# Weight subtractions, index lookup and the pace of routing in a two-layer encoder kernel

## The chip, the core and the metric

The kernel runs on one core of one Trainium2 chip, as one program without loops. The metric is the device time of one execution in microseconds (us); the time given is the median of the timed runs. Engines are named as in the profile: PE (TensorE, matrix products), PEld (its weight loads), DVE (VectorE), ACT (ScalarE), POOL (GpSimd) and SP (which issues the DMA loads of weights).

## What is computed

Two layers over 256 tokens of width 1024. Each layer runs four kinds of attention on the tokens (the *mixers*) and then a feed-forward part called PEER, which picks experts by keys. The change lies almost wholly in PEER:

```python
def peer_ffn(u, wq, keys, u_tab, v_tab):
    q = (u @ wq).reshape(b, s, PEER_HEADS, 2, PEER_DKEY // 2)
    scores = jnp.einsum('bshpk,hpnk->bshpn', q, keys).astype(jnp.float32)
    sub_s, sub_i = lax.top_k(scores, PEER_TOPK)
    cand_s = (sub_s[..., 0, :, None] + sub_s[..., 1, None, :]).reshape(...)
    cand_i = (sub_i[..., 0, :, None] * PEER_NKEYS + sub_i[..., 1, None, :]).reshape(...)
    top_s, pos = lax.top_k(cand_s, PEER_TOPK)
    eidx = jnp.take_along_axis(cand_i, pos, axis=-1)
    gates = jax.nn.softmax(top_s, axis=-1)
    ...
        h = jax.nn.gelu(jnp.einsum('td,thkd->thk', ut, ue).astype(jnp.float32), approximate=False)
        w = (gt * h).astype(ut.dtype)
        return jnp.einsum('thk,thkd->td', w, v_tab[it])
```

There are 8 heads, 128 keys on each of two sides (so 16384 experts), and 16 experts are kept per head and token.

## The kernel before

**Split products.** Every float32 product with a weight is made of three products in a faster format: a value is split into `hi` and `lo`, and hi x hi, lo x hi and hi x lo are added. `stream` (L102) loads one weight block of 128 x 1024 into `raw` (three buffers, `raw_load` L91), ACT writes `hi` (L97), and an engine subtracts, `lo = raw - hi` (L98). `hi` and `lo` have three buffers each. Which engine subtracts is decided in `stream`: `share["every"]` is 0 in the mixers (always DVE), 3 in routing and in the output sum (every third block goes to POOL) and 2 in gating (every second block):

```python
        eng = eng or (G if share["every"] and share["n"] % share["every"] == 0 else V)
```

`w_out_blocks` (L774) splits eight blocks of the attention's output weight per layer, four of them with POOL (`wol`).

**PEER in three stages** (`peer`, L833). The kernel doesn't gather experts. It computes the hidden value of all 16384 experts, 128 tiles of 128, and sets the gate of those not chosen to zero.

1. *Routing* (`routing` L852). A call of `hidden` (L996) computes two tiles of experts: two weight blocks of `in_pu`, 24 matmuls of 256 columns each (L288 to L290). Between the calls stand steps of routing: `project` and `score` for 16 pairs of head and side (tile `sc`), then `top16` of 128 scores (L1110 to L1115, into `subs` and `iu`, from there to `subi`), and then, for each half `t` of the tokens, 100 candidate sums per head (`cand`), `top16` of them (`tops`, `pos`), the *lookup* and a softmax. Each step yields a cost. A loop (L1016 to L1023) adds a credit of 3.2 per call of `hidden` and hands out steps until the credit is used up. The costs before are 2.6 for the first projection, `CH` = 1.1 for each of 16 projections, 1.0 for each of 32 top-16, and per half of the tokens twice 0.6, eight times 0.9, 0.5, four times 1.7 + 1.1, 0.5 and 0.5. The costs only set the order in which the program is written; they are no waits.
2. *Lookup*, the part of routing that turns positions among candidates into key numbers (L930 to L941): a position's 4-bit index is compared with 0 to 15 (tile `oh`, one-hot, L933), multiplied by the 16 kept key numbers `subi` (L939) and summed over the 16 (L941, into `res`). One pass does one side for four heads, so there are four passes of 128 x 1024 per half.
3. *Gating* (`gating` L961). For eight tokens at a time it compares both key numbers with 0 to 127 (`a`, L976; `e`, L978) and multiplies `e` by the gates (`b`, two times, L980). PE multiplies `a` and `b` (L985, tile `pC`, eight short matmuls of 128 columns for a batch of four tokens), which gives the gate of each expert; DVE multiplies these into the hidden values `ha` and `hb` (L990), and ACT copies the rest. The 64 batches are spread over the calls of `hidden` that routing left.

After them comes the *output sum* (from L1042): 128 blocks of `in_pv`, split in the same way, twelve matmuls of 512 columns each into `y` (L113 to L115), in the first layer with the next layer's conditioning (`araw`, L152, on DVE) in between.

**What sets the order.** Each engine runs its own list of instructions in order and waits on semaphores. A scheduler places the instructions by the order in which they are written and by its own estimates. A DVE instruction that waits holds up every one behind it, `lo` included.

Of the kernel before, what the change touches and what calls it, by code (L numbers as in the profile page):

```python
# [9 lines left out]
F32 = mybir.dt.float32  # L10
F32R = mybir.dt.float32r
BF = mybir.dt.bfloat16
# [18 lines left out]
GT = 8  # L31
CH = 1.1
GSTEP = 1
BSTEP = 1
GSCALE = 2.0 ** 14


@with_exitstack
def kernel(ctx, tc, T, out):
# [34 lines left out]
    G.iota(iota, pattern=[[1, 128]], base=0, channel_multiplier=0, allow_small_or_imprecise_dtypes=True)  # L74
    iota4 = const([128, 16, 4], BF, "iota4")
    V.tensor_copy(iota4, iota[:, 0:16][:, :, None].to_broadcast([128, 16, 4]))
    mhalf = const([128, 16], F32, "mhalf")
# [21 lines left out]

    share, state = {"every": 0, "n": 0}, {}  # L100

    def stream(src, w=1024, eng=None):  # L102

        raw = raw_load(src, w)
        share["n"] += 1
        eng = eng or (G if share["every"] and share["n"] % share["every"] == 0 else V)
        hi = sp.tile([128, 1024], F32R, name="hi")
        lo = sp.tile([128, 1024], F32R, name="lo")
        split(hi[:, :w], lo[:, :w], raw[:, :w], eng)
        return hi, lo  # L110
# [272 lines left out]
    def mixers(l, u, begun):  # L383
        mpool = tc.tile_pool(name="mix", reuse_waits="tile", bufs=1)
        mx = mpool.__enter__()
        share["every"] = 0
        lambda_init = 0.8 - 0.6 * math.exp(-0.3 * l)
# [386 lines left out]
        with tc.tile_pool(name="mout", reuse_waits="tile", bufs=1) as op:  # L774
            wo = {}

            def w_out_blocks():
                for hh, b in [(hh, b) for b in range(3) for hh in range(2)] + [(0, 3), (1, 3)]:
                    raw = op.tile([128, 1024], F32, name="wraw", bufs=2)
                    nc.sync.dma_start(raw, T["wout"][l, hh, b])  # L780
                    hi = op.tile([128, 1024], F32R, name=f"woh{hh}{b}")
                    lo = op.tile([128, 1024], F32R, name=f"wol{hh}{b}")
                    split(hi, lo, raw, G if b % 2 else V)
                    wo[hh, b] = hi, lo
                    yield
# [49 lines left out]
    def peer(l, u, begun):  # L835
# [16 lines left out]
        def routing(rp):  # L852

            subs = [rp.tile([128, 16, 16], F32, name=f"subs{t}", bufs=1) for t in range(2)]
            subi = [rp.tile([128, 16, 16], BF, name=f"subi{t}", bufs=1) for t in range(2)]
            def project(c):
                if c % 8 == 0:
                    state["keys"] = rp.tile([128, 1024], F32, name="keys", bufs=1)
                    nc.gpsimd.dma_start(state["keys"], T["keys"][l, c // 8])
                if c % 4 == 0:  # L860
                    state["sc"] = [psA("sc").rearrange("p (h n) -> p h n", h=4) for _ in range(2)]
                p = psA()
                if c < 4:
                    for t in range(2):
                        transpose(p[:, t * 128:(t + 1) * 128], qa[:, t, c * 128:(c + 1) * 128])
                else:
                    proj_b(p[:, :S], T["wq"][l, c - 4], u, 8)
                qs = rp.tile([128, S], F32, name="qs")
                A.activation(qs, p[:, :S], AF.Copy)
                return qs  # L870
# [11 lines left out]
            for g in range(4):  # L882
                qs = project(g * 4)
                for i in range(1, 4):
                    yield CH
                    nqs = project(g * 4 + i)
                    score(g * 4 + i - 1, qs)
                    qs = nqs
                yield CH
                score(g * 4 + 3, qs)  # L890
                for t in range(2):
                    iu = rp.tile([128, 4, 16], U32, name="iu")
                    for i in range(4):
                        top16(rp, subs[t][:, g * 4 + i, :], iu[:, i, :], state["sc"][t][:, i, :], 128)
                        yield 1.0
                    V.tensor_copy(subi[t][:, g * 4:g * 4 + 4, :], iu)
            for t in range(2):
# [3 lines left out]
                for h in range(8):  # L901
                    if h % 4 == 0:
# [8 lines left out]
                                        s1[:, :, 0:4][:, :, None, :].to_broadcast([128, 4, 13, 4]), op=ALU.add)  # L911
                        yield 0.6
                    top16(rp, tops[:, h, :], pos[:, h, :], cand[:, h % 4, :], 100)
                    yield 0.9
                au = rp.tile([128, 3, 128], U32, name="au", bufs=1)
# [11 lines left out]
                res = rp.tile([128, 4, 128], F32, name="res", bufs=1)  # L927
                yield 0.5
                for q in range(2):
                    for h4 in range(2):  # L930
                        ks = slice(h4 * 64, h4 * 64 + 64)
                        oh = rp.tile([128, 16, 64], BF, name="oh16", bufs=1)
                        V.tensor_tensor(oh.rearrange("p a (k i) -> p a k i", i=4),  # L933
                                        iota4[:, :, None, :].to_broadcast([128, 16, 16, 4]),
                                        af[:, q, ks].rearrange("p (k i) -> p k i", i=4)[:, None, :, :]
                                        .to_broadcast([128, 16, 16, 4]), op=ALU.is_equal)
                        si = subi[t][:, q::2, :][:, h4 * 4:h4 * 4 + 4, :].rearrange("p h a -> p a h")
                        o4 = oh.rearrange("p a (h k) -> p a h k", h=4)
                        V.tensor_tensor(o4, o4, si[:, :, :, None].to_broadcast([128, 16, 4, 16]), op=ALU.mult)  # L939
                        yield 1.7  # L940
                        V.tensor_reduce(res[:, q, ks], oh.rearrange("p a k -> p k a"), axis=AX.X, op=ALU.add)  # L941
                        yield 1.1
                gv = res[:, 2, :].rearrange("p (h k) -> p h k", h=8)
                V.tensor_tensor(gv, tops, tops[:, :, 0:1].to_broadcast([128, 8, 16]), op=ALU.subtract)
                A.activation(gv, gv, AF.Exp)
                yield 0.5
                gs = rp.tile([128, 8], F32, name="gs")
# [11 lines left out]
                A.activation(rt[:, :, t * 128:(t + 1) * 128], p, AF.Copy)  # L959
                yield 0.5  # L960

# [50 lines left out]
        with tc.tile_pool(name="route", reuse_waits="tile", bufs=2) as rp:  # L1012
            steps, credit = routing(rp), 0.0
            share["every"] = 3
            while steps is not None and state["tiles"] < 128:
                hidden(None)  # L1016
                credit += 3.2 if share["every"] else 2.6
                while credit > 0:
                    c = next(steps, None)
                    if c is None:  # L1020
                        steps = None
                        break
                    credit -= c  # L1023
            if steps is not None:
                for _ in steps:
                    pass
        share["every"] = 2
        with tc.tile_pool(name="gp", reuse_waits="tile", bufs=2) as gp:
# [13 lines left out]
        last = l + 1 == L  # L1042
        share["every"] = 3
        yps = [[psA(f"y{t}{h}") for h in range(2)] for t in range(2)]
# [166 lines left out]
```

## Time and profile before

| | us |
|---|---|
| median of three timed runs | 2518.3 (2515.56 to 2518.84) |
| profiled execution | 2525.81, of it span 2524.0 |
| PE busy | 2390.5 (95%) |
| DVE busy | 1842.1 (73%) |
| ACT busy | 1207.5 (48%) |
| POOL busy | 652.1 (26%) |

A busy time adds up the instructions of an engine. PE's matmuls overlap, so "busy" says that it never stood still, not that it ran at its best pace. Idle time counts against a waiting instruction only after the one before it has ended. In the trace the second layer begins near 1300 us. Its routing runs from about 1680 to 1920, its gating to 2152 and its output sum to 2515; in the first layer routing runs from about 440 to 673, gating to 885, the output sum to 1300.

### The profile page before, as it was taken

The numbers are of one execution on the slowest core, as the hardware profiler recorded it, in microseconds if no ns is written. First come the engines' busy times: TensorE is split into PE (matmuls) and PEld (weight loads), VectorE is DVE, ScalarE is ACT, GpSimd is POOL, SyncE is SP. The second block draws the span as 40 slices with busy tenths as digits, with TensorE's granted clock in tenths as the row PEclk, the third lists the DMA queues.
The fourth block names the chain that finished last, engine by engine and source line by source line (L and its number), as shares of the span: only waits on it lengthen the run. The fifth ranks groups of instructions, "written<-read, shape, count | busy, mean of one in ns | idle before, by whom it ended". The sixth has DMA issues, their size and how long they took to land. (4 is left out here: it accounts for less than half of the span.)

```text
span 2524.0 us, 41444 instructions
## 1 busy us (share of the span) xinstructions
PE 2390.5 (95%) x15844; PEld 2134.6 (85%) x15844; DVE 1842.1 (73%) x3190; ACT 1207.5 (48%) x2114; POOL 652.1 (26%) x348
## 2 busy tenths in 40 slices
PE   7989998998999999899989999999989999999997
PEld 4779987998999988777768899879979999788886
DVE  7766667559899968677577665756798998555556
ACT  3654553444444445445446554734444544444453
POOL 2111012222233333233311110212223334233231
PEclk9999999999999999999999999999999999999999
DMA  8666564554455478787654455635544544566664
GB/s 274 193 179 209 166 215 144 185 176 151 151 160 152 142 253 272 231 277 252 198 163 125 145 159 159 226 109 186 166 137 160 159 151 154 177 189 194 192 214 145
DMA packets 141255, 459.97 MB, mean 182 GB/s; under 512 B 27472, under 2 KB 27488, under 8 KB 141056
## 3 DMA queue, kind: packets, MB, share of 16 engines
q1 hardware_dynamic: 135776, 439.93, 55.1%
q0 software_dynamic: 4848, 16.34, 2.0%
q8 instruction: 124, 2.03, 0.3%
q10 hardware_dynamic: 432, 1.05, 0.1%
q14 instruction: 75, 0.61, 0.1%
HBM read 453.05 MB, written 4.21 MB: 181 GB/s over the span
## 5 line engine op out<-in xcount | busy, mean ns | idle before, releaser
L97 ACT ACTIVATE hi<-raw 128x1024 fp32r<-128x1024 f32 (+2 forms) x705 | 737.8, 1052 | 557.3 <-PE pA L289 163.6
L98 DVE TENSOR_TENSOR lo<-raw,hi 128x1024 fp32r<-128x1024 f32 (+2 forms) x505 | 634.1, 1257 | 305.7 <-ACT hi L97 304.9
L98 POOL TENSOR_TENSOR lo<-raw,hi 128x1024 fp32r<-128x1024 f32 x200 | 507.4, 2537 | 1137.1 <-ACT hi L97 1112.2
L290 PE MATMUL pB<-uh,lo 128*128 128x256 f32 x2048 | 585.7, 286 | 24.8 <-DVE lo L98 24.2
L288 PE MATMUL pB<-uh,hi 128*128 128x256 f32 x2048 | 587.4, 287 | 0.3 <-ACT hi L97 0.3
L289 PE MATMUL pB<-ul,hi 128*128 128x256 f32 x2048 | 580.6, 283 | 0.0
L290 PEld LDWEIGHTS pB<-uh,lo 128*128 128x128 f32 x2048 | 389.1, 190 | 31.5 <-DVE lo L98 27.5
L113 PE MATMUL y<-hi,wh 128*128 128x512 f32 x968 | 385.2, 398 | 12.4 <-ACT hi L97 7.1
L114 PE MATMUL y<-lo,wh 128*128 128x512 f32 x968 | 382.4, 395 | 12.3 <-DVE lo L98 6.5
L288 PEld LDWEIGHTS pB<-uh,hi 128*128 128x128 f32 x2048 | 389.4, 190 | 0.6 <-ACT hi L97 0.5
L289 PEld LDWEIGHTS pB<-ul,hi 128*128 128x128 f32 x2048 | 389.4, 190 | 0.1
L115 PE MATMUL y<-hi,wl 128*128 128x512 f32 x968 | 384.0, 397 | 0.7 <-DVE wl L98 0.7
L98 DVE TENSOR_TENSOR wl<-ha,wh 128x256 fp32r<-128x256 f32 x220 | 146.1, 667 | 171.7 <-ACT wh L97 171.4
L288 PE MATMUL pA<-uh,hi 128*128 128x256 f32 x832 | 240.3, 289 | 0.0
L290 PE MATMUL pA<-uh,lo 128*128 128x256 f32 x832 | 238.5, 287 | 0.9 <-DVE lo L98 0.9
L289 PE MATMUL pA<-ul,hi 128*128 128x256 f32 x832 | 238.3, 286 | 0.0
L114 PEld LDWEIGHTS y<-lo,wh 128*128 128x128 f32 x968 | 184.6, 191 | 56.1 <-DVE lo L98 8.7
L113 PEld LDWEIGHTS y<-hi,wh 128*128 128x128 f32 x968 | 184.5, 191 | 52.3 <-ACT hi L97 8.4
L115 PEld LDWEIGHTS y<-hi,wl 128*128 128x128 f32 x968 | 184.5, 191 | 42.5 <-DVE wl L98 1.5
L97 ACT ACTIVATE wh<-ha 128x256 fp32r<-128x256 f32 x220 | 91.3, 417 | 266.4 <-PE y L114 264.2
L290 PEld LDWEIGHTS pA<-uh,lo 128*128 128x128 f32 x832 | 158.4, 190 | 2.2 <-DVE lo L98 1.1
L288 PEld LDWEIGHTS pA<-uh,hi 128*128 128x128 f32 x832 | 158.5, 191 | 0.7
(312 smaller groups left out, 3646.8 us busy)
## 6 DMA issues: line engine op xcount, KB each, us to landing
raw<-in_pu_dram SPq DMA_DIRECT2D x256, 512.0 KB, 3.6
raw<-in_pv_dram SPq DMA_DIRECT2D x256, 512.0 KB, 4.4
araw<-in_ada_w_dram SPq DMA_DIRECT2D x80, 512.0 KB, 4.9
raw<-in_wgate_dram SPq DMA_DIRECT2D x64, 512.0 KB, 3.6
raw<-in_win_a_dram SPq DMA_DIRECT2D x48, 512.0 KB, 3.7
raw<-in_wbr_dram SPq DMA_DIRECT2D x32, 512.0 KB, 3.8
raw<-in_wq_dram SPq DMA_DIRECT2D x24, 512.0 KB, 3.7
aw<-in_ada_w_dram SPq DMA_DIRECT2D x32, 256.0 KB, 5.8
```

The costliest lines, as they stand in the source:

```text
L97: A.activation(hi, src, AF.Copy)
L98: (eng or V).tensor_tensor(lo, src, hi.bitcast(F32), op=ALU.subtract)
L113: PE.matmul(o, sh, mh, start=first, stop=False)
L114: PE.matmul(o, sh, ml, start=False, stop=False)
L115: return PE.matmul(o, sl, mh, start=False, stop=last).ins
L288: PE.matmul(o[:, ts], hi[:, ws], uh[:, kc, ts], start=kc == 0, stop=False)
L289: PE.matmul(o[:, ts], hi[:, ws], ul[:, kc, ts], start=False, stop=False)
L290: end = PE.matmul(o[:, ts], lo[:, ws], uh[:, kc, ts], start=False, stop=kc == nk - 1)
```

## The change

1. `stream` has no `share` any more: all its blocks are subtracted by DVE, except two at the very start of the program that are given to POOL by name. `w_out_blocks` does the same.
2. The lookup does one side for all eight heads in one pass of 128 x 2048. The key numbers lie twice, side by side, in `subi`, and `iu` is filled in another order, so that the multiply reads pairs. The sum over 16 is made of four additions on halves, the first three in bf16. `oh` shares its memory with `keys`.
3. The credit per call of `hidden` is `RSTEP` = 3.7, and the steps have other costs.

```diff
-CH = 1.1
+CH = 0.3
+RSTEP = 3.7
+OHC = 1.2
-    iota4 = const([128, 16, 4], BF, "iota4")
+    iota16 = const([128, 16, 16], BF, "iota16")
 def stream(src, w=1024, eng=None):
-        share["n"] += 1
-        eng = eng or (G if share["every"] and share["n"] % share["every"] == 0 else V)
 def w_out_blocks():
-                    split(hi, lo, raw, G if b % 2 else V)
+                    split(hi, lo, raw)
 def routing(rp):
-            subi = [rp.tile([128, 16, 16], BF, name=f"subi{t}", bufs=1) for t in range(2)]
+            subi = [rp.tile([128, 2, 128, 2], BF, name=f"subi{t}", bufs=1) for t in range(2)]
-                        top16(rp, subs[t][:, g * 4 + i, :], iu[:, i, :], state["sc"][t][:, i, :], 128)
-                        yield 1.0
-                    V.tensor_copy(subi[t][:, g * 4:g * 4 + 4, :], iu)
+                        top16(rp, subs[t][:, g * 4 + i, :], iu[:, i % 2 * 2 + i // 2, :], state["sc"][t][:, i, :], 128)
+                        yield 1.7
+                    V.tensor_copy(subi[t][:, :, g * 32:g * 32 + 32, :],
+                                  iu.rearrange("p (q h) a -> p q (h a)", q=2)[:, :, :, None]
+                                  .to_broadcast([128, 2, 32, 2]))
-                        yield 0.6
+                        yield 1.7
                     top16(rp, tops[:, h, :], pos[:, h, :], cand[:, h % 4, :], 100)
-                    yield 0.9
+                    yield 1.5
-                yield 0.5
+                yield 1.6
                 for q in range(2):
-                    for h4 in range(2):
-                        ks = slice(h4 * 64, h4 * 64 + 64)
-                        oh = rp.tile([128, 16, 64], BF, name="oh16", bufs=1)
-                        V.tensor_tensor(oh.rearrange("p a (k i) -> p a k i", i=4),
-                                        iota4[:, :, None, :].to_broadcast([128, 16, 16, 4]),
-                                        af[:, q, ks].rearrange("p (k i) -> p k i", i=4)[:, None, :, :]
-                                        .to_broadcast([128, 16, 16, 4]), op=ALU.is_equal)
-                        si = subi[t][:, q::2, :][:, h4 * 4:h4 * 4 + 4, :].rearrange("p h a -> p a h")
-                        o4 = oh.rearrange("p a (h k) -> p a h k", h=4)
-                        V.tensor_tensor(o4, o4, si[:, :, :, None].to_broadcast([128, 16, 4, 16]), op=ALU.mult)
-                        yield 1.7
-                        V.tensor_reduce(res[:, q, ks], oh.rearrange("p a k -> p k a"), axis=AX.X, op=ALU.add)
-                        yield 1.1
+                    oh = rp.tile([128, 8, 16, 16], BF, name="oh16", tag="keys", bufs=1)
+                    V.tensor_tensor(oh, iota16[:, None, :, :].to_broadcast([128, 8, 16, 16]),
+                                    af[:, q, :].rearrange("p (h k) -> p h k", h=8)[:, :, None, :]
+                                    .to_broadcast([128, 8, 16, 16]), op=ALU.is_equal)
+                    yield OHC
+                    ov = oh.rearrange("p h a (k i) -> p (h a) k i", i=2)
+                    V.tensor_tensor(ov, ov, subi[t][:, q, :, None, :].to_broadcast([128, 128, 8, 2]), op=ALU.mult)
+                    yield OHC
+                    for n in (8, 4, 2):
+                        V.tensor_tensor(oh[:, :, :n, :], oh[:, :, :n, :], oh[:, :, n:2 * n, :], op=ALU.add)
+                    V.tensor_tensor(res[:, q, :].rearrange("p (h k) -> p h k", h=8), oh[:, :, 0, :], oh[:, :, 1, :],
+                                    op=ALU.add)
+                    yield OHC
-                yield 0.5
+                yield 0.8
...
-                yield 0.5
+                yield 2.0
 # the loop over routing and hidden
-            share["every"] = 3
-                credit += 3.2 if share["every"] else 2.6
+                credit += RSTEP
-        share["every"] = 2
```

How the order of instructions moves is seen at three places. In these rows a name is a tile, the numbers behind it tell buffers apart, and the line numbers are those of each kernel itself.

POOL's list, first layer, from the end of the attention part (`zs`) to the loads for the end of PEER (`xr`). Before:

```order
L236 DMA xd_93<-zs 128x1024
L89 TENSOR_TENSOR brs<-rs_in,mhalf 128x1
L98 TENSOR_TENSOR lo<-raw,hi 128x1024
L859 DMA keys<-in_keys_dram 128x1024
L98 TENSOR_TENSOR lo<-raw,hi 128x1024 x6
L859 DMA keys<-in_keys_dram 128x1024
L98 TENSOR_TENSOR lo<-raw,hi 128x1024 x69
L142 DMA grow_102<-cols 128x8x1
L98 TENSOR_TENSOR lo<-raw,hi 128x1024 x16
L142 DMA grow_103<-cols 128x8x1
L98 TENSOR_TENSOR lo<-raw,hi 128x1024 x2
L213 DMA xr_13170<-xd_93 128x1024
```

After:

```order
L236 DMA xd_93<-zs 128x1024
L91 TENSOR_TENSOR brs<-rs_in,mhalf 128x1
L860 DMA keys<-in_keys_dram 128x1024 x2
L142 DMA grow_102<-cols 128x8x1
L142 DMA grow_103<-cols 128x8x1
L213 DMA xr_13160<-xd_93 128x1024
L213 DMA xr_13163<-xd_93 128x1024
```

The 94 subtractions `lo` of this stretch are gone from POOL's list; what is left are loads, and the small `brs` of the layer norms.

DVE's list in gating, first layer, one cycle in steady state. Before:

```order
L978 TENSOR_TENSOR e_8155<-iota_7276,rt 128x1024
L98 TENSOR_TENSOR lo<-raw,hi 128x1024
L1009 TENSOR_TENSOR ha<-ha,gel 128x2x56
L990 SCALAR_TENSOR_TENSOR ha<-pC,ha 128x74x4 x2
L976 TENSOR_TENSOR a_8151<-iota_7276,rt 128x1024
L980 TENSOR_TENSOR b_8152<-e_8155,rt 128x1024
L980 TENSOR_TENSOR b_8153<-e_8155,rt 128x1024
L978 TENSOR_TENSOR e_8252<-iota_7276,rt 128x1024
```

After:

```order
L982 TENSOR_TENSOR e_8113<-iota_7396,rt 128x1024
L100 TENSOR_TENSOR lo<-raw,hi 128x1024
L1013 TENSOR_TENSOR ha<-ha,gel 128x2x48
L994 SCALAR_TENSOR_TENSOR ha<-pC,ha 128x76x4 x2
L980 TENSOR_TENSOR a_8109<-iota_7396,rt 128x1024
L984 TENSOR_TENSOR b_8110<-e_8113,rt 128x1024
L984 TENSOR_TENSOR b_8111<-e_8113,rt 128x1024
L100 TENSOR_TENSOR lo<-raw,hi 128x1024
L982 TENSOR_TENSOR e_8210<-iota_7396,rt 128x1024
```

There are now two `lo` in a cycle, one on either side of the compare `e`, where one stood before.

DVE's list in the lookup, first layer, first half of the tokens. Before, two of the four passes:

```order
L933 TENSOR_TENSOR oh_6519<-iota_88,af 128x1024
L1113 MATCH_REPLACE mrep<-tops,cand 128x100
L939 TENSOR_TENSOR oh_6519<-oh_6519,subi_4601 128x1024
L948 TENSOR_REDUCE gs<-res 128x8
L941 TENSOR_REDUCE res<-oh_6519 128x64
L98 TENSOR_TENSOR lo<-raw,hi 128x1024
L933 TENSOR_TENSOR oh_6523<-iota_88,af 128x1024
L949 RECIPROCAL gs<-gs 128x8
L939 TENSOR_TENSOR oh_6523<-oh_6523,subi_4601 128x1024
L98 TENSOR_TENSOR lo<-raw,hi 128x1024
L941 TENSOR_REDUCE res<-oh_6523 128x64
```

After, one of the two passes (the last addition, L944 into `res`, is the row that follows):

```order
L935 TENSOR_TENSOR oh_6643<-iota_88,af 128x2048
L100 TENSOR_TENSOR lo<-raw,hi 128x1024
L940 TENSOR_TENSOR oh_6643<-oh_6643,subi_4601 128x2048
L952 TENSOR_REDUCE gs<-res 128x8
L100 TENSOR_TENSOR lo<-raw,hi 128x1024
L943 TENSOR_TENSOR oh_6643<-oh_6643 128x8x128
L953 RECIPROCAL gs<-gs 128x8
L943 TENSOR_TENSOR oh_6643<-oh_6643 128x8x64
L954 TENSOR_SCALAR gs<-gs 128x8
L1115 MAX tops<-mrep 128x8
L943 TENSOR_TENSOR oh_6643<-oh_6643 128x8x32
L955 TENSOR_TENSOR res<-res,gs 128x128
```

The multiply and compare are twice as long, L941 with its sum over 16 has become L943 and L944, and `lo` stands between most steps.

## Rows read from the trace of the kernel before

**Rows 1.** The page: busy time (1), clock granted in 40 slices (2).

```profile
PE 2390.5 (95%) x15844; PEld 2134.6 (85%) x15844; DVE 1842.1 (73%) x3190; ACT 1207.5 (48%) x2114; POOL 652.1 (26%) x348
...
PEclk9999999999999999999999999999999999999999
```

**Rows 2.** Stretches: length; PE, PEld, DVE, ACT, POOL busy (instructions); clock, DMA, GB/s.

```profile
560.00:673.00 113.00, 102.23 (x819) 100.38 (x818) 102.72 (x272) 49.69 (x59) 30.51 (x11) 0.97 0.49 155
673.00:885.00 212.00, 209.00 (x1963) 204.95 (x1961) 209.77 (x255) 95.16 (x231) 78.53 (x30) 1.00 0.49 150
885.00:1262.00 377.00, 357.51 (x1616) 293.27 (x1615) 269.73 (x284) 180.39 (x262) 115.18 (x50) 0.97 0.76 247
1690.00:1810.00 120.00, 120.00 (x1009) 119.63 (x1009) 69.35 (x256) 54.26 (x71) 31.67 (x14) 1.00 0.59 186
1810.00:1920.00 110.00, 96.16 (x772) 94.27 (x772) 101.09 (x254) 47.15 (x57) 28.27 (x11) 0.97 0.45 150
1920.00:2152.00 232.00, 227.25 (x2119) 222.87 (x2117) 220.86 (x267) 105.91 (x247) 88.13 (x34) 1.00 0.49 154
```

**Rows 3.** Groups by line: busy, mean ns | idle just before, what ended it.

```profile
L290 PE MATMUL pB<-uh,lo 128*128 128x256 f32 x2048 | 585.7, 286 | 24.8 <-DVE lo L98 24.2 <-POOL lo L98 0.5
...
L114 PE MATMUL y<-lo,wh 128*128 128x512 f32 x968 | 382.4, 395 | 12.3 <-DVE lo L98 6.5 <-POOL lo L98 5.7
```

**Rows 4.** Time line of a lookup: start, us, instruction [idle before].

```profile
599.38 3.37 POOL L98 TENSOR_TENSOR lo<-raw,hi 128x1024 fp32r<-128x1024 f32 x1 [7.96 <-ACT hi L97]
...
600.54 3.30 DVE L939 TENSOR_TENSOR oh<-oh,subi 128x1024 bf16<-128x1024 bf16 x1
...
603.76 1.21 DVE L98 TENSOR_TENSOR lo<-raw,hi 128x1024 fp32r<-128x1024 f32 x1
...
605.03 0.39 PE L290 MATMUL pB<-uh,lo 128*128 128x256 f32 x1 [1.96 <-DVE lo L98]
```

**Rows 5.** Time line of gating, second layer, DVE but for three rows.

```profile
1958.00 2.56 POOL L98 TENSOR_TENSOR lo<-raw,hi 128x1024 fp32r<-128x1024 f32 x1 [4.04 <-ACT hi L97]
...
1958.35 2.75 DVE L978 TENSOR_TENSOR e<-iota,rt 128x1024 f16<-128x1024 f16 x1
1961.03 1.21 DVE L98 TENSOR_TENSOR lo<-raw,hi 128x1024 fp32r<-128x1024 f32 x1
...
1964.98 2.77 DVE L978 TENSOR_TENSOR e<-iota,rt 128x1024 f16<-128x1024 f16 x1
...
2059.80 0.87 PE L985 MATMUL pC<-b,a 128*128 128x128 f16 x12
...
2066.70 1.11 PE L985 MATMUL pC<-b,a 128*128 128x128 f16 x16
...
2083.00 2.77 DVE L978 TENSOR_TENSOR e<-iota,rt 128x1024 f16<-128x1024 f16 x1
...
2090.24 2.76 DVE L978 TENSOR_TENSOR e<-iota,rt 128x1024 f16<-128x1024 f16 x1
...
2099.72 0.69 DVE L978 TENSOR_TENSOR e<-iota,rt 128x1024 f16<-128x1024 f16 x1
```

**Rows 6.** Groups by line and form, DVE, and POOL's `lo`.

```profile
L98 DVE TENSOR_TENSOR lo<-raw,hi 128x1024 fp32r<-128x1024 f32 x491 | 620.3, 1264 | 302.7 <-ACT hi L97 301.8
L978 DVE TENSOR_TENSOR e<-iota,rt 128x1024 f16<-128x1024 f16 x64 | 146.8, 2294 | 2.0
...
L976 DVE TENSOR_TENSOR a<-iota,rt 128x1024 f16<-128x1024 f16 x64 | 45.5, 712 | 0.1
L941 DVE TENSOR_REDUCE res<-oh 128x64 f32<-128x1024 bf16 x16 | 32.4, 2023 | 0.1
...
L939 DVE TENSOR_TENSOR oh<-oh,subi 128x1024 bf16<-128x1024 bf16 x16 | 21.5, 1346 | 0.0
...
L933 DVE TENSOR_TENSOR oh<-iota,af 128x1024 bf16<-128x1024 bf16 x16 | 11.1, 693 | 0.1
...
L98 POOL TENSOR_TENSOR lo<-raw,hi 128x1024 fp32r<-128x1024 f32 x200 | 507.4, 2537 | 1137.1 <-ACT hi L97 1112.2 <-PE pB L289 10.2 <-PE pC L985 8.6
```

More of the change, by code (lines that the diff above doesn't have):

```diff
@@ L74 @@
     G.iota(iota, pattern=[[1, 128]], base=0, channel_multiplier=0, allow_small_or_imprecise_dtypes=True)
-    iota4 = const([128, 16, 4], BF, "iota4")
-    V.tensor_copy(iota4, iota[:, 0:16][:, :, None].to_broadcast([128, 16, 4]))
+    iota16 = const([128, 16, 16], BF, "iota16")
+    V.tensor_copy(iota16, iota[:, 0:16][:, :, None].to_broadcast([128, 16, 16]))
     mhalf = const([128, 16], F32, "mhalf")
@@ L98, in split @@
         (eng or V).tensor_tensor(lo, src, hi.bitcast(F32), op=ALU.subtract)
-    share, state = {"every": 0, "n": 0}, {}
+    state = {}
     def stream(src, w=1024, eng=None):
         raw = raw_load(src, w)
-        share["n"] += 1
-        eng = eng or (G if share["every"] and share["n"] % share["every"] == 0 else V)
         hi = sp.tile([128, 1024], F32R, name="hi")
@@ L385, in mixers @@
         mx = mpool.__enter__()
-        share["every"] = 0
         lambda_init = 0.8 - 0.6 * math.exp(-0.3 * l)
@@ L854, in routing @@
             subs = [rp.tile([128, 16, 16], F32, name=f"subs{t}", bufs=1) for t in range(2)]
-            subi = [rp.tile([128, 16, 16], BF, name=f"subi{t}", bufs=1) for t in range(2)]
+            subi = [rp.tile([128, 2, 128, 2], BF, name=f"subi{t}", bufs=1) for t in range(2)]
             def project(c):
                 if c % 8 == 0:
-                    state["keys"] = rp.tile([128, 1024], F32, name="keys", bufs=1)
+                    state["keys"] = rp.tile([128, 1024], F32, name="keys", tag="keys", bufs=1)
                     nc.gpsimd.dma_start(state["keys"], T["keys"][l, c // 8])
@@ L1042, in peer @@
         last = l + 1 == L
-        share["every"] = 3
         yps = [[psA(f"y{t}{h}") for h in range(2)] for t in range(2)]
```

## Prediction

> **What bounds the kernel now.** I read the page's busy shares first: TensorE is busy 95% of the span, its granted clock full nearly everywhere [rows 1]. A gain can only come from places where TensorE waits or runs at its lower level. The table by stage shows them [rows 2]. In 1690 to 1810 us, the first half of routing in the second layer, TensorE is never idle and starts 1009 matmuls in 120 us, 118.9 ns each: its pace with 256 columns and no wait. Against that pace:
>
> - Lookup of indices (560 to 673 and 1810 to 1920): 819 and 772 matmuls need 97.4 and 91.8 us and took 113 and 110. Lost: 15.6 + 18.2 = **33.8 us**. The granted clock averages 0.97 here, so idle time is not all of it.
> - Gating (673 to 885 and 1920 to 2152): VectorE is busy 209.8 of 212 and 220.9 of 232 us. Of the 1963 and 2119 matmuls 512 each are short gating ones. Sixteen of those take 1.11 us, twelve 0.87 [rows 5]: between (1.11 - 0.87) / 4 = 0.06 and 0.069 us each. The stages need 203.2 and 221.8 us by the one, 208.0 and 226.6 by the other. Lost: **9 to 19 us** together.
> - Output sum, first layer (885 to 1262): TensorE is idle 19.5 of 377 us, and a clock of 0.97 costs another 11.
>
> Next, who made it wait. The page's groups name `lo` by VectorE, 24.2 us ahead of the hidden-layer products, and `lo` by VectorE and GpSimd, 6.5 and 5.7 us, ahead of the output sum [rows 3]. The time line of one lookup shows what stood behind a late `lo` [rows 4]: GpSimd begins a subtraction at 599.38 and ends at 602.75; VectorE's multiply, begun at 600.54, takes 3.30 us where the mean is 1.35 [rows 6]; the `lo` queued behind it comes at 603.76, and TensorE takes it up at 605.03 after 1.96 us of nothing. Gating shows it in step [rows 5]: GpSimd subtracts from 1958.00 to 1960.56, and the compare `e`, begun at 1958.35, lasts 2.75 us. With no subtraction beside it the same compare takes 0.69 (2099.72). The mean of all 64 is 2.29, that of its twin `a`, of the same size, 0.71 [rows 6]. So a subtraction on GpSimd makes VectorE stand for about 2.1 us; VectorE itself does one in 1.21 us [rows 5].
>
> **The change part by part.**
>
> *Subtractions.* 198 of the 200 `lo` on GpSimd and 8 `wol` move. VectorE gets 206 x 1.26 = 260 us more work [rows 6] and no longer stands: for `e` alone 64 x (2.29 - 0.71) = 101 us, and up to 2 us for each of the other 134. GpSimd's `lo` took 2.54 us, so a third to a half of all `lo` are also ready 1.3 us sooner and free their raw buffer for the next load.
>
> *Gating.* VectorE's cycle for one call of the hidden layer was 6.63 us early (1958.35 to 1964.98) and 7.24 late (2083.00 to 2090.24), with one `lo` on it and one on GpSimd [rows 5]. Now: less 2.06 for `e`, plus 1.21 for the second `lo`: 5.8 to 6.4. The step costs of one half of the tokens add up to 2 x 1.7 + 8 x 1.5 + 1.6 + 6 x 1.2 + 0.8 + 2.0 = 27 (before: 21.1), those of all routing to 2.6 + 16 x 0.3 + 32 x 1.7 + 2 x 27 = 115.8 (before: 94.4). At 3.7 and 3.2 a call that is 32 calls and 30, so of 64 calls 32 are left for the 64 batches instead of 34, and VectorE's cycle grows to 6.0 to 6.6. TensorE's own is 48 x 0.1189 + 16 x 0.06 = 6.7, and that is next. Gain per cycle: (6.63 + 7.24) / 2 - 6.67 = 0.27, 64 cycles, 17 us; within the bounds above I take **15**.
>
> *Lookup.* Before, for one half of the tokens: 4 x (0.693 + 1.346 + 2.023) = 16.2 us [rows 6]. After, twice per half: a compare and a multiply over 2048 elements and four additions of 1024, 512, 256 and 128 results. The compare is double L933: 1.2 to 1.4. The multiply on doubled index pairs is not in the trace: from above 2 x 1.346 = 2.7, from below 1.2, if it goes like the compares, whose gating form also reads pairs (0.71 for 1024). I take 1.3, since it is nearest to those. The additions: 0.69 for the first, for the others between their share of it and the same again, 1.3 to 2.8, taken 1.5. Per half 2 x 4.1 = 8.2 us, up to 13.8; VectorE saves 8 us four times.
>
> In the two stretches together VectorE is busy 203.8 us [rows 2]. Less 32; plus 22 subtractions of GpSimd's at 1.26, 27.7; less their standing still, 0 to 45. The pace goes along: a half was 21.1 at 3.2 a call, 6.6 calls, and is 27 at 3.7, 7.3 calls, so 11% more of TensorE's work stands beside it, 189.2 becomes 210, with 11% more `lo` (1591 / 24 = 66 blocks, so 7), 9 us. VectorE: 163 to 208, TensorE 210. At worst level. Three buffers let VectorE run two blocks ahead; I leave 5 of the 33.8 us for bunched instructions: gain **29**.
>
> The Trainium skill speaks against the chain of additions: "VectorE: DVE Perf Modes", section on the TRN2 errata, says each instruction pays a fixed extra and wants tiles of 512 elements or more. By its measured fixed term of about 150 cycles the four would take 1.7 us instead of 1.5, an estimate from that page; the eight chains would cost VectorE 2 us more, and the sum nothing that shows. No row of this trace has such a chain.
>
> *First half of routing.* Projections come four in a row (step cost 0.3 for 1.1). The burst of 14 top-16 instructions that stands ahead of the next `lo` is the same before and after in the order, and TensorE lost nothing to it [rows 2], with three blocks of split weights as its cover. I cost it at nothing. Without that cover a gap like that at 605.03 [rows 4] at each of 8 groups of heads costs 16 us.
>
> *Output sum.* The 5.7 us ahead of GpSimd's `lo` go, and half of the 6.5 ahead of VectorE's, which is no longer held up. VectorE has room, 270 of 377 us. The rest of the idle time I take for loads and leave. Gain **9**, from 0 (loads are late anyway) to 20.
>
> *W_out's `wol`*, the constants and `iu`'s new places: nothing, within 3 us either way, hidden under gate products that TensorE works on then.
>
> Sum: 29 + 15 + 9 = **53 us**. The profiled execution took 2525.8 us, its span 2524.0; the median of the timed runs is 0.3% lower, 2518.3. 2518.3 - 53 = **2465 us**.
>
> **The rivals.**
>
> 1. *Half of it.* All `lo` now stand in one queue, behind lookup instructions and behind the `araw` products, which wait for loads of their own. For it: VectorE may be level with TensorE in the lookup. Against: in the output sum it has 107 us to spare. Lookup 15, gating 10, output 0: 2493 us.
>
> 2. *Slower: VectorE becomes the bound of gating.* This decides if `e` was long for a reason of its own, not because GpSimd ran. Then the second `lo` comes on top of a full engine: 6.94 + 1.21 = 8.15 us a cycle, 1.21 more than today, 64 times, 77 us; less 29 and 9 it ends 39 us slower, 2557 us. From an `e` of about 2.1 us on (5.40 + e = 6.94 + 38 / 64) the whole is slower. Against it stands the 0.69 of 2099.72. The Trainium skill ("Perfetto Trace Analysis", Optimizing Scalar/DVE Operations) leans to this side: where VectorE is saturated, giving work to GpSimd may make sense, and gating is busy 95 to 99%. The same paragraph warns that the two share a read port and that it might not help; rows 5 agree with the warning, at 2.75 against 0.69 us.
>
> 3. *Nothing.* The lost time is loads, and VectorE was the last to be ready by chance: 2513 to 2523. Against: rows 4 and 5 have a GpSimd subtraction beside each instruction that came late.
>
> 4. *More.* With no waits the clock stays up too, and the output sum loses 20 us less: 33 + 19 + 20 = 72, 2446 us.
>
> **How the numbers follow.** Forecast 0.60, half 0.20, more 0.10, slower 0.06, nothing 0.04. Range 2442 to 2494, from rival 4 to rival 1. Some 0.2%, 5 us, is what a measurement of this kernel can tell from no change: faster 0.90, same 0.04, slower 0.06.
>
> **What would show it.** `e` at 0.7 us; 703 `lo` on VectorE at 1.2; VectorE busy under 97% in gating; the lookup's multiply at 1.3 us for 2048 elements; TensorE's waits for `lo` ahead of the hidden layer under 8 us, with the clock full through both lookups. It is wrong if gating's cycle stays near 7 us, if the multiply takes 2.7, or if waits for `lo` turn up in the first half of routing or grow in the output sum.

## The result, and the profile after

The changed kernel takes **2460.75 us** (2456.81 to 2468.10), the kernel before 2518.57 beside it: ratio 0.9778, 95% interval 0.9758 to 0.9799, 57.8 us less. The forecast was 2465, range 2442 to 2494. The profiled execution of the changed kernel took 2456.81 us, its span 2455.0, 69 us less than the profiled one of before.

Busy time on the page, against [rows 1]: TensorE 18 us less, GpSimd 527 less.

```profile
PE 2372.4 (97%) x15844; PEld 2116.3 (86%) x15844; DVE 1803.0 (73%) x3394; ACT 1211.2 (49%) x2108; POOL 125.3 (5%) x142
```

VectorE got 206 subtractions of 1.235 us more, 254 us; its lookup got 32 us cheaper (65.0 us in [rows 6], 32.8 below). Its busy time still fell by 39. So about 254 + 39 - 32 = 261 us of the old busy time were VectorE standing, 1.3 us for each subtraction that GpSimd had. The groups by line and form, as in [rows 3, 6]:

```profile
L100 DVE TENSOR_TENSOR lo<-raw,hi 128x1024 fp32r<-128x1024 f32 x689 | 849.1, 1235 | 368.2 <-ACT hi L99 367.5
L982 DVE TENSOR_TENSOR e<-iota,rt 128x1024 f16<-128x1024 f16 x64 | 43.7, 683 | 0.2
L935 DVE TENSOR_TENSOR oh<-iota,af 128x2048 bf16<-128x2048 bf16 x8 | 9.7, 1218 | 0.1
L940 DVE TENSOR_TENSOR oh<-oh,subi 128x2048 bf16<-128x2048 bf16 x8 | 9.7, 1216 | 0.0
L943 DVE TENSOR_TENSOR oh<-oh 128x1024 bf16<-128x1024 bf16 x8 | 5.5, 685 | 0.0
L943 DVE TENSOR_TENSOR oh<-oh 128x512 bf16<-128x512 bf16 x8 | 3.3, 418 | 0.0
L943 DVE TENSOR_TENSOR oh<-oh 128x256 bf16<-128x256 bf16 x8 | 2.3, 283 | 0.0
L944 DVE TENSOR_TENSOR res<-oh 128x128 f32<-128x128 bf16 x8 | 2.3, 284 | 0.0
...
L290 PE MATMUL pB<-uh,lo 128*128 128x256 f32 x2048 | 579.6, 283 | 1.6 <-DVE lo L100 1.6
L114 PE MATMUL y<-lo,wh 128*128 128x512 f32 x968 | 384.9, 398 | 7.0 <-DVE lo L100 7.0
```

`e` takes 0.68 us instead of 2.29; the waits for `lo` ahead of the hidden layer went from 24.8 to 1.6 us, those ahead of the output sum from 12.3 to 7.0. The stages, with the columns of [rows 2] (lookup, gating and output sum of the first layer, then first half of routing, lookup, gating and output sum of the second):

```profile
558.00:664.00 106.00, 105.20 (x878) 104.53 (x877) 93.69 (x287) 53.35 (x63) 0.00 (x0) 1.00 0.53 180
664.00:879.00 215.00, 214.72 (x2048) 212.81 (x2045) 191.17 (x295) 104.88 (x239) 0.00 (x0) 1.00 0.47 158
879.00:1259.00 380.00, 368.89 (x1584) 294.87 (x1584) 272.05 (x338) 181.61 (x261) 6.00 (x9) 0.99 0.75 253
...
1650.00:1755.00 105.00, 105.00 (x883) 105.00 (x882) 73.95 (x247) 45.92 (x58) 0.54 (x1) 1.00 0.55 186
...
1762.00:1868.00 106.00, 105.15 (x881) 104.54 (x880) 93.75 (x287) 53.43 (x63) 0.00 (x0) 1.00 0.52 179
1868.00:2083.00 215.00, 214.43 (x2044) 212.52 (x2041) 190.93 (x295) 104.93 (x239) 0.00 (x0) 1.00 0.47 158
2082.00:2446.00 364.00, 361.60 (x1541) 289.35 (x1540) 216.87 (x270) 175.27 (x257) 3.56 (x6) 0.99 0.55 188
```

Priced as in the prediction (118.9 ns a matmul, 0.06 us a short one): the lookups need 878 x 0.1189 = 104.4 and 104.8 us and took 106, so they lose 2.8 us instead of 33.8. Gating needs 1536 x 0.1189 + 512 x 0.06 = 213.3 and 212.9 and took 215, so it loses 3.8 us. By the same price it lost 16.4 before, and not 19, since two stretches of [rows 2] have the wrong ends: 673 to 885 ends with the last short product, but the hidden layer goes on to 903, and 1920 to 2152 takes in 2 us in which no matmul starts. Cut where the hidden layer ends, gating before needed 1607 x 0.1189 + 512 x 0.06 = 221.8 us and took 230, twice, and the first output sum runs from 903 to 1293. Before, with these ends (gating and output sum of the first layer, gating of the second):

```profile
673.00:903.00 230.00, 227.00 (x2119) 222.78 (x2117) 218.33 (x265) 104.34 (x245) 87.14 (x34) 1.00 0.50 153
903.00:1293.00 390.00, 369.10 (x1586) 299.09 (x1586) 282.77 (x296) 184.67 (x261) 110.16 (x49) 0.97 0.76 247
...
1920.00:2150.00 230.00, 226.97 (x2119) 222.80 (x2117) 220.19 (x266) 104.36 (x245) 88.13 (x34) 1.00 0.49 153
```

VectorE is busy 89% in gating now, and it waits for TensorE. The time line of VectorE in one cycle of gating, against [rows 5]: from `a` to `a` 6.69 us, with 0.85 idle ahead of `b` until the product `pC` is done.

```profile
732.68 0.68 DVE L980 TENSOR_TENSOR a<-iota,rt 128x1024 f16<-128x1024 f16 x1
...
734.96 1.22 DVE L100 TENSOR_TENSOR lo<-raw,hi 128x1024 fp32r<-128x1024 f32 x1
736.10 0.68 DVE L982 TENSOR_TENSOR e<-iota,rt 128x1024 f16<-128x1024 f16 x1
736.70 1.22 DVE L100 TENSOR_TENSOR lo<-raw,hi 128x1024 fp32r<-128x1024 f32 x1
738.76 0.69 DVE L984 TENSOR_TENSOR b<-e,rt 128x1024 f16<-128x1024 f16 x1 [0.85 <-PE pC L989]
739.37 0.68 DVE L980 TENSOR_TENSOR a<-iota,rt 128x1024 f16<-128x1024 f16 x1
```

### The profile page after: what moved, and what is told of

Same layout as the page of the kernel before. It is cut to its first block, busy times and chain, and to the rows that moved or that the text cites. A ratio compares the mean times of both kernels' runs of the same rounds, so it can differ in the third digit from the quotient of the medians.

```text
span 2455.0 us, 41405 instructions
## 1 busy us (share of the span) xinstructions
PE 2372.4 (97%) x15844; PEld 2116.3 (86%) x15844; DVE 1803.0 (73%) x3394; ACT 1211.2 (49%) x2108; POOL 125.3 (5%) x142
## 5 line engine op out<-in xcount | busy, mean ns | idle before, releaser
L100 DVE TENSOR_TENSOR lo<-raw,hi 128x1024 fp32r<-128x1024 f32 (+1 forms) x703 | 862.9, 1230 | 371.3 <-ACT hi L99 370.6
L290 PE MATMUL pB<-uh,lo 128*128 128x256 f32 x2048 | 579.6, 283 | 1.6 <-DVE lo L100 1.6
L100 DVE TENSOR_TENSOR wl<-ha,wh 128x256 fp32r<-128x256 f32 x220 | 92.8, 423 | 98.4 <-ACT wh L99 98.3
L289 PEld LDWEIGHTS pA<-ul,hi 128*128 128x128 f32 x832 | 158.1, 190 | 0.7
```

The lines of the kernel that those rows point to most:

```text
L100: (eng or V).tensor_tensor(lo, src, hi.bitcast(F32), op=ALU.subtract)
L289: PE.matmul(o[:, ts], hi[:, ws], ul[:, kc, ts], start=False, stop=False)
L290: end = PE.matmul(o[:, ts], lo[:, ws], uh[:, kc, ts], start=False, stop=kc == nk - 1)
```

## Experiments 1: each part alone, and all but one

The theory (A): what was lost was VectorE standing while GpSimd subtracts. The rival (B): the new lookup and the new pace bring the gain, or a good part of it.

**subs_only**: the kernel before, with this alone.

```diff
-        eng = eng or (G if share["every"] and share["n"] % share["every"] == 0 else V)
+        eng = eng or V
-                    split(hi, lo, raw, G if b % 2 else V)
+                    split(hi, lo, raw)
```

> The kernel before with the first part of the change alone: every weight subtraction of stream and w_out_blocks on VectorE; old lookup, old step costs and pace. Theory A (a GpSimd subtraction makes VectorE stand for some 2 us, and that was the loss): gating falls by 12 to 16 us, the output sum by about 9, the lookup by about half of its 33.8 us since VectorE (204 us there, less its standing still, plus 28 us of new subtractions) stays near TensorE's 189: about 2480 us, e at 0.7 us. Theory B (the gain comes from the new lookup and the new pace): nothing or slower, 2515 us or more, because VectorE gets 260 us of work.

**lookup_only**: the kernel before with `iota16`, the paired `subi`, one pass for eight heads and the four additions. In the diff, only its ends:

```diff
-    iota4 = const([128, 16, 4], BF, "iota4")
+    iota16 = const([128, 16, 16], BF, "iota16")
-                        V.tensor_reduce(res[:, q, ks], oh.rearrange("p a k -> p k a"), axis=AX.X, op=ALU.add)
+                    for n in (8, 4, 2):
+                        V.tensor_tensor(oh[:, :, :n, :], oh[:, :, :n, :], oh[:, :, n:2 * n, :], op=ALU.add)
```

> The kernel before with the second part alone: one pass per side for eight heads with doubled index pairs and four additions; GpSimd's share, old pace (the lookup's step costs add up to the same 11.2 per half of the tokens). Theory A: only the lookup gains, VectorE has 32 us less in two stretches of 113 and 110 us where TensorE lost 33.8: 15 to 20 us, about 2500 us, with e still at 2.3 us and gating unchanged. Theory B: the lookup's whole loss goes, 2485 to 2490 us.

**pace_only**: the kernel before with the new costs.

```diff
-CH = 1.1
+CH = 0.3
-                credit += 3.2 if share["every"] else 2.6
+                credit += 3.7
```

> The kernel before with the third part alone: credit 3.7 a call and the new step costs, with the old lookup's eight steps at 0.9 so that one half of the tokens costs the same 27. Theory A: lookup and gating are together bound by VectorE, whose work stays the same, so calls that move from gating to routing bring nearly nothing: 2510 to 2518 us. Theory B: the lookup has 11% more of TensorE's work beside it and loses less, 10 to 15 us: 2503 to 2508 us.

**share_back**: the changed kernel with the lines of the first diff put back.

> The changed kernel with the first part undone: every third block in routing and output sum, every second one in gating and half of W_out's blocks go back to GpSimd; new lookup and new pace stay. Theory A: gating is VectorE's again and has two calls fewer to cover it, e at 2.3 us or more, the output sum loses its 9 us, some of the lookup's gain stays: 2495 to 2505 us, so 35 to 45 of the 58 us are lost. Theory B: it keeps most of the gain, 2461 to 2476 us.

| kernel | us (median) | ratio to before, 95% interval |
|---|---|---|
| subs_only | 2462.6 | 0.9781 (0.9765 to 0.9797) |
| lookup_only | 2519.62 | 1.0007 (0.9989 to 1.0025) |
| pace_only | 2523.79 | 1.0020 (1.0008 to 1.0031) |
| share_back | 2523.05 | 1.0008 (0.9995 to 1.0021) |

The subtractions alone bring all of it; the other two parts together bring nothing without them. B is out as the source of the gain. But A's sizes were off as well: 17 us too little for the subtractions, 20 too much for the lookup, and share_back lost all 62 us where A had 35 to 45. (lookup_only and share_back also have the larger constant `iota16`, to which Experiments 4 come back.) The lookups and first gating of subs_only:

```profile
557.00:659.00 102.00, 98.26 (x795) 96.36 (x794) 101.07 (x281) 48.37 (x56) 0.00 (x0) 0.98 0.52 163
659.00:882.00 223.00, 222.65 (x2119) 221.04 (x2118) 196.96 (x302) 107.95 (x245) 0.00 (x0) 1.00 0.50 160
...
1767.00:1869.00 102.00, 98.19 (x793) 96.25 (x792) 101.04 (x281) 48.59 (x57) 0.00 (x0) 0.98 0.51 163
```

They lose 7.5 + 7.7 = 15.2 us here, 18.6 less than before, and gating 1.2 of 223 with the old pace: 1607 x 0.1189 + 512 x 0.06 = 221.8. In lookup_only the lookups did get 7 us better, though some of the additions there stand for GpSimd as well (418 and 283 ns for these forms in the changed kernel):

```profile
562.00:668.00 106.00, 98.92 (x791) 97.28 (x790) 89.29 (x272) 48.08 (x56) 27.91 (x11) 0.97 0.48 157
1795.00:1904.00 109.00, 99.75 (x792) 98.71 (x791) 93.79 (x272) 48.09 (x56) 30.93 (x11) 0.95 0.48 156
```

```profile
L942 DVE TENSOR_TENSOR oh<-oh 128x256 bf16<-128x256 bf16 x8 | 8.8, 1103 | 0.0
L942 DVE TENSOR_TENSOR oh<-oh 128x512 bf16<-128x512 bf16 x8 | 7.5, 932 | 0.0
```

Lost are 106 - 94.0 and 109 - 94.2, 26.8 us instead of 33.8. Yet the median did not move. The second output sum took longer, 371 us for 1542 matmuls, where it had been 365 for 1539.

## Experiments 2: does anything come on top of the subtractions?

**after_again** and **subs_again** are the changed kernel and subs_only once more; **subs_lookup** and **subs_pace** are subs_only with the diff of lookup_only or of pace_only. All four ran on one chip. A and B mean something else in their expectations: the lookups of the whole change lose 12 us less than those of subs_only, and by A that shortens the program, by B it is given back elsewhere.

> The changed kernel once more, on the chip of the next three. Alone, the subtractions reached 2462.6 us where the whole change had 2460.75. In the profiled pair the lookups of the whole lose 4.1 us of TensorE's time and those of the subtractions alone 16.3. Theory A (these 12 us are real and shorten the program): 2450 to 2456 us if the subtractions alone repeat 2462. Theory B (they are given back elsewhere, in the output sum or at the clock): 2459 to 2462 us.

> The subtractions alone, repeated beside the whole change. Both theories: 2460 to 2465 us; A has it 8 to 12 us above the whole change on the same chip, B within 4 us.

> Subtractions on VectorE and the new lookup, with the old step costs and the pace of 3.2. Theory A: the new lookup took 7 us from the lookups when it came alone, and takes as much here: 16 us of loss become about 9, gating stays at its 4.4: 5 to 8 us below the subtractions alone, 2454 to 2457 us. Theory B: within 3 us of them.

> Subtractions on VectorE and the new step costs with the pace of 3.7; the old lookup, its eight steps at 0.9. Theory A: VectorE is no longer the bound of gating, so the calls that move into the lookup cover more of it: its 16 us of loss become 8 to 12, gating loses 1 to 2 us more: 3 to 6 us below the subtractions alone. Theory B: within 3 us of them, or above, as the pace alone was (2523.8 against 2519.0 us).

| kernel | us (median) | ratio to before, 95% interval |
|---|---|---|
| after_again | 2461.06 | 0.9775 (0.9759 to 0.9790) |
| subs_again | 2464.66 | 0.9792 (0.9775 to 0.9809) |
| subs_lookup | 2459.93 | 0.9768 (0.9749 to 0.9787) |
| subs_pace | 2462.61 | 0.9775 (0.9760 to 0.9790) |

The four can't be told apart. In the lookups they differ clearly, though; here subs_lookup, then subs_pace:

```profile
560.00:656.00 96.00, 95.06 (x796) 94.20 (x795) 88.41 (x283) 48.71 (x57) 0.00 (x0) 1.00 0.56 176
```

```profile
558.00:670.00 112.00, 107.95 (x881) 105.53 (x880) 107.79 (x286) 53.60 (x62) 0.00 (x0) 1.00 0.52 170
```

The new lookup takes the loss down to 96 - 94.6 = 1.4 us, the new pace leaves it at 112 - 104.8 = 7.2. So on top of the subtractions the new lookup is worth 12 us in two lookups, the pace next to nothing; and the 12 us are given back somewhere, as B has it. Where they go shows in stretches of 100 us inside the second output sum, where nothing waits: before, subs_again, after_again, subs_lookup.

```profile
2250.00:2350.00 100.00, 100.00 (x439) 82.13 (x438) 51.31 (x60) 49.55 (x73) 29.51 (x13) 1.00 0.62 193
```

```profile
2191.00:2291.00 100.00, 100.00 (x438) 82.06 (x437) 60.09 (x74) 50.27 (x74) 0.00 (x0) 1.00 0.58 190
```

```profile
2188.00:2288.00 100.00, 100.00 (x431) 80.56 (x429) 59.14 (x72) 48.83 (x72) 0.00 (x0) 1.00 0.58 188
```

```profile
2189.00:2289.00 100.00, 100.00 (x430) 80.56 (x430) 59.08 (x72) 48.98 (x72) 0.00 (x0) 1.00 0.58 188
```

TensorE is busy all the time at the full clock in each, yet it does 438 or 439 matmuls where the old lookup is, 430 or 431 where the new one is. Without the two at the edges that is 229 and 233 ns from one to the next.

## Experiments 3: a GpSimd instruction that nobody waits for

A late `lo` could also have been late because GpSimd takes 2.5 us for it (theory C), not because VectorE stands. **gp_two** is the changed kernel with this behind the compare `a` in gating; **gp_one** has `G.tensor_copy(junk, af8)` in its place.

```diff
                     V.tensor_tensor(a8, iq, q[0], op=ALU.is_equal)
+                    junk = gp.tile([128, 1024], F16, name="junk", bufs=1)
+                    af8 = a8.rearrange("p g i t -> p (g i t)")
+                    G.tensor_tensor(junk, af8, af8, op=ALU.subtract)
```

> The changed kernel with one more GpSimd instruction for every eight tokens of gating, 64 in all: it subtracts the tile a from itself (two operands in SBUF) into a tile that nobody reads, and it can start when a is written, just as the compare e starts. No product waits for it. Theory A (a GpSimd subtraction makes VectorE stand): e goes from 0.68 to between 2.0 and 2.8 us, VectorE's cycle from 6.0 to 7.3 or more against TensorE's 6.72, gating is VectorE's again: 40 to 90 us slower than the change, 2500 to 2550 us. Theory C (what was lost was the wait for a lo that GpSimd makes in 2.5 us instead of 1.2): e stays at 0.7 us and the time within 5 us of the change.

> As the kernel with the added GpSimd subtraction, but the added instruction is a copy of a, one operand. If any GpSimd instruction on SBUF makes VectorE stand: e as there, over 1.5 us. If it takes two operands in SBUF to do so, as theory A reads the row of before: e below 1.0 us and the time within 10 us of the change, 2460 to 2470 us. Theory C: within 5 us of the change here too.

gp_two: 2520.22 us, ratio to before 1.0005 (0.9991 to 1.0020). 64 instructions without a reader give back the whole gain, with every `lo` still on VectorE. gp_one: 2469.3 us, 0.9797 (0.9773 to 0.9821), some 8 us above the change. So C is out in gating. In the output sum it is not: 5.7 of the 12.3 us of waits before ended with a `lo` of GpSimd's own [rows 3], and no run tells there whether GpSimd was late or VectorE. It was not `e` that stood (0.76 us on average): the added instruction begins as soon as `a` is written, but in VectorE's list `ha` and `b` follow `a`, and `e` comes after them. Against the changed kernel `b` took 49 us more in all, `lo` 29, `a` and `e` 9. Rows of gp_two: groups, the first gating stretch, and a piece of the time line.

```profile
L290 PE MATMUL pB<-uh,lo 128*128 128x256 f32 x2048 | 587.2, 287 | 20.1 <-DVE lo L100 19.8
L983 POOL TENSOR_TENSOR junk<-a 128x1024 f16<-128x1024 f16 x64 | 155.2, 2426 | 646.6 <-DVE a L980 646.6
L987 DVE TENSOR_TENSOR b<-e,rt 128x1024 f16<-128x1024 f16 x128 | 133.7, 1066 | 4.9 <-PE pC L992 3.7
```

```profile
664.00:909.00 245.00, 224.69 (x2043) 220.02 (x2040) 232.89 (x296) 102.18 (x238) 77.36 (x31) 0.97 0.43 139
```

```profile
734.71 0.90 DVE L997 SCALAR_TENSOR_TENSOR ha<-pC,ha 128x328 f32<-128x328 f32 x2
734.71 1.90 POOL L983 TENSOR_TENSOR junk<-a 128x1024 f16<-128x1024 f16 x1 [4.79 <-DVE a L980]
...
735.52 1.62 DVE L987 TENSOR_TENSOR b<-e,rt 128x1024 f16<-128x1024 f16 x1
```

GpSimd is done at 736.61; `b`, begun at 735.52, ends 0.53 us after that, where it takes 0.68 in all when alone. The `ha` products beside the same instruction take what they always take: one of their operands, `pC`, lies in PSUM. In gp_one GpSimd's copy is shorter and reads one tile, and `b` stands for less. By its expectation gp_one would say that it takes two operands on GpSimd (`e` 0.71 us, less than 10 us above the change), but that looked at `e` alone; `b` takes 0.82 us on average instead of 0.68:

```profile
L982 POOL COPY junk<-a 128x1024 f16<-128x1024 f16 x64 | 109.2, 1706 | 644.5 <-DVE a L980 644.5
L986 DVE TENSOR_TENSOR b<-e,rt 128x1024 f16<-128x1024 f16 x128 | 102.7, 824 | 11.2 <-PE pC L991 10.0
```

## Experiments 4: where the weight tiles lie

`iota16` takes 512 bytes a partition among the constants, `iota4` took 128. By the order in which the program lays out its tiles, all that comes behind them (`raw`, `hi`, `lo`, `uh`, `ul`, `ha`, `hb`) moves up by 384 bytes; `wh` and `wl`, laid out from the other end, stay. Two kernels take the place apart from the lookup. **after_place** is the changed kernel with

```diff
-    iota16 = const([128, 16, 16], BF, "iota16")
+    hole = const([128, 32], F32, "hole")
     upool = ctx.enter_context(tc.tile_pool(name="upool", bufs=1))
+    late = ctx.enter_context(tc.tile_pool(name="late", bufs=1))
+    iota16 = late.tile([128, 16, 16], BF, name="iota16")
```

and **subs_shift** is subs_only with

```diff
+    pad = const([128, 96], F32, "pad")
     mhalf = const([128, 16], F32, "mhalf")
```

> The changed kernel with iota16 (512 bytes a partition) placed behind upool instead of among the constants, and 128 bytes left where it was, as many as iota4 took. So raw, hi, lo, uh and ul lie at the addresses that they have in the kernel before; the change has them 384 bytes higher. In the three profiled runs with the new lookup and all subtractions on VectorE (after, after_again, subs_lookup) the 512-column matmuls of the output sums start 233.3 ns apart, in the three with the old lookup (subs_only, subs_again, subs_pace) 229.0 on average. Theory P (the place of the weight tiles sets that pace): 229.0 ns, 3104 x 4.3 ns = 13 us less in the output sums, 2446 to 2450 us. Theory Q (the new lookup does it in another way, by what it leaves of loads or of the order): 233.3 ns and 2459 to 2463 us.

> The subtractions alone with the old lookup, and a constant of 384 bytes a partition that nothing reads, ahead of the weight tiles: raw, hi and lo lie where the change has them. Theory P: 233.3 ns between the 512-column matmuls, 13 us longer than the subtractions alone, 2475 to 2478 us. Theory Q: 229.0 ns and 2461 to 2465 us.

| kernel | us (median) | ratio to before, 95% interval |
|---|---|---|
| after_place | 2451.89 | 0.9742 (0.9721 to 0.9763) |
| subs_shift | 2472.70 | 0.9826 (0.9804 to 0.9848) |

The same stretch of after_place, then of subs_shift:

```profile
2186.00:2286.00 100.00, 100.00 (x439) 82.05 (x438) 60.13 (x73) 49.51 (x73) 0.00 (x0) 1.00 0.60 192
```

```profile
2197.00:2297.00 100.00, 100.00 (x430) 80.56 (x430) 58.72 (x72) 49.24 (x72) 0.00 (x0) 1.00 0.58 187
```

Theory P, that the place of the weight tiles sets the pace, holds in both directions: the old place gives 439 with the new lookup, the new place 430 with the old one. after_place has the lowest median of all kernels here, 9 us below the changed one, though the intervals touch; subs_shift is 8 to 10 above subs_only and subs_again. At the old place, then, the new lookup and pace are worth 10 to 13 us on top of the subtractions, and the move takes most of that away. The 13 us that P foretold came only in part: the first output sum, where TensorE also waits for loads, is 378 us long in after_place (1586 matmuls) and 381 in after_again (1586), the second one 358 and 362.

## Why the prediction was right, and where it was not

The time was right within 5 us, and the cause named for it, GpSimd's subtractions holding up VectorE, is shown by subs_only, share_back and gp_two. Which part of the change earns what was not right.

- **Lookup, 29 us forecast:** 33.8 - 2.8 = 31.0. The prediction gave the new lookup 32 us of relief on VectorE and called the rest standing, without saying what either alone would do. Measured: 18.6 by the subtractions, 12 more by the new lookup. VectorE was busy 187 us in the two stretches (forecast 163 to 208), which are 212 us long. The prices of the pieces held: compare 1.218 (1.2 to 1.4), multiply 1.216 (taken 1.3; it does go like the compare). The four additions took 685 + 418 + 283 + 284 = 1.67 us, where I took 1.5; the estimate of 1.7 by the Trainium skill ("VectorE: DVE Perf Modes", section on the TRN2 errata) was the better one.
- **Gating, 15 us:** 16.4 - 3.8 = 12.6 at the lower price of a short product. The higher one, 0.069 us, is out: by it gating would now need 218.2 us and takes 215. The prediction's 19 us of loss was too much by the wrong ends of its two stretches. VectorE's work in a cycle is 5.8 us, just under the forecast 6.0 to 6.6, as I had left `b` at its old 0.87 (0.68 now). TensorE is next, as said. The pace has no part in it: with 30 calls in routing (subs_only) gating loses 1.2 us a layer.
- **Output sum, 9 us:** 10 in the first layer (390 us for 1586 matmuls, now 380 for 1584) and 1 in the second (365, now 364). The sum is near by luck, for two terms cancel. Waits fell by more: with the old place of the tiles the two sums are 18 us shorter in subs_only and 24 in subs_again. Against it stands the slower row of matmuls, 3100 x 4.3 ns = 13 us, which no step had. The step that failed is "*W_out's `wol`*, the constants [...]: nothing": the constants were priced by the work on them, not by what they push along.
- **First half of routing, 0:** right, 105 us for 883 matmuls, 118.9 ns each, with no gap.
- **W_out, 0 within 3 us:** `ol`, which reads two tiles in SBUF beside GpSimd's `wol`, went from 1.10 to 0.68 us and TensorE's waits around it from 6.4 to 4.2. In the second layer the products with W_out go through some 4 us faster. About what was said.
- **The rest.** Of the 69 us between the two profiled executions 55 are in the first three of these stages. The other 14 lie mostly in the attention parts, where one kernel's executions differ by several us too. The profiled execution of before was 7 us above its median, that of the change 4 below; between the medians 58 us are left, near the 55 of the terms.
- **Rivals.** "Half" needed VectorE level with TensorE in the lookup, but it was busy 187 of 212 us. "Nothing" is out with subs_only. "Slower" needed an `e` of 2.1 us or more for its own reason; it took 0.68. gp_two shows the other side of that sum: once VectorE is held up again, gating takes 245 us for 215 and the gain is gone. "More" (2446) is what after_place comes near to, by another way than the one given.

Open: why the pace of the 512-column matmuls depends on the place, and whether `hi` and `lo`, which they read, or another of the shifted tiles decides. after_place narrows it down: `ha` and `hb`, laid out behind the moved constant, are not back at their old place there, and the old pace returned all the same. Each of the 14 profiled executions falls on the side of its place, but only two places were run.

## What to carry to other kernels

Before work is shared with GpSimd, look up what VectorE's instructions take beside it and alone; a helper that makes the saturated engine stand for longer than the work it takes over is worth removing, whatever its own busy share. Judge each part of a change on its own: here one line had the gain, and a second part's gain was paid back by a constant that moved the weights. When a change adds or resizes anything laid out ahead of large tiles, count the matmuls in a stretch without waits before and after.

## What the runs showed of the hardware

- **Who stands.** Beside GpSimd's subtraction, VectorE instructions that read two tensors in SBUF (`e`, `b`, `acc`, and `wl`, 0.67 us on average before and 0.42 now) grew. In the trace of before, a sum over 16, with one operand, runs its usual 2.07 us beside it (mean 2.02), and a top-16 instruction its 0.28:

```profile
647.49 2.51 POOL L98 TENSOR_TENSOR lo<-raw,hi 128x1024 fp32r<-128x1024 f32 x1 [7.87 <-ACT hi L97]
647.65 2.07 DVE L941 TENSOR_REDUCE res<-oh 128x64 f32<-128x1024 bf16 x1
```

```profile
1740.14 2.42 POOL L98 TENSOR_TENSOR lo<-raw,hi 128x1024 fp32r<-128x1024 f32 x1
1740.25 0.28 DVE L1114 MAX8 subs<-mrep 128x8 f32<-128x128 f32 x1
```

That fits the bursts of top-16 in the first half of routing, which had cost TensorE nothing [rows 2]. But one tensor is not always safe: the copy of `iu` into `subi`, which also changes the type, reads a single one. It takes 0.18 to 0.20 us alone, and beside a subtraction it ended with it:

```profile
471.30 2.38 POOL L98 TENSOR_TENSOR lo<-raw,hi 128x1024 fp32r<-128x1024 f32 x1 [5.88 <-ACT hi L97]
472.67 1.07 DVE L896 CAST subi<-iu 128x64 bf16<-128x64 uint32 x1
```

On average this copy took 0.56 us before and 0.19 in subs_only. It goes the other way too: where VectorE's multiply and `lo` were there first, GpSimd's subtraction took 4.22 us and ended 2.25 us after that `lo`.

```profile
612.99 1.22 DVE L939 TENSOR_TENSOR oh<-oh,subi 128x1024 bf16<-128x1024 bf16 x1
613.38 4.22 POOL L98 TENSOR_TENSOR lo<-raw,hi 128x1024 fp32r<-128x1024 f32 x1 [10.63 <-ACT hi L97]
614.13 1.22 DVE L98 TENSOR_TENSOR lo<-raw,hi 128x1024 fp32r<-128x1024 f32 x1
```

For two tensors the Trainium skill has this as a rule ("SBUF — State Buffer", section Who interferes with whom): a VectorE instruction with two SBUF inputs and a GpSimd instruction that reads SBUF exclude each other, and the first to come keeps the port to its end. The traces agree, with 1.62 against 0.68 us for `b`, and gp_one shows that one operand on GpSimd's side is enough.

- **The place of tiles.** 384 bytes change the spacing of the output sum's 512-column matmuls from 229 to 233 ns, with TensorE busy throughout and the clock full. The 256-column ones don't show it: gating takes 222 to 223 us for 2116 to 2122 matmuls in subs_only, subs_shift and subs_lookup alike.
